# Loading the last tile whole and finishing it in four pieces, in a streaming gradient kernel

## Chip, cores, metric

One core of a Trainium2 chip. The metric is the device time of one execution in microseconds (us). A run more than 1.5% above the fastest of its kernel counts as slow. The experiments ran in three rounds, each on another chip; a ratio compares only runs of one round, while the profiles are compared across them.

## The reference

```python
def setup_inputs():
    return {"x": np.random.randn(8192, 8192).astype(np.float32)}

def reference(x):
    return np.gradient(x, axis=1)
```

Inside a row each result is half the difference of the two neighbours; at the two ends it is the plain difference. 268 MB are read and 268 MB written, with one operation per element: a streaming kernel.

## The kernel before

A tile is two rows per partition, 64 KB per partition and 8 MB in all. There are 32 tiles (0 to 31) and three buffers. SyncE issues the loads, ScalarE the stores, but for those of the last tile, which SyncE issues. GpSimd computes the row ends aside (0.2 us), VectorE does the middle in one instruction (17.2 us), shifted by 64 elements inside the same buffer, and a small copy puts the ends in place. Only the last tile is handled in two rows:

```python
parts = [(ld[k], 0, R)] if i < nsets - 1 else [(ld_rows[r], r, 1) for r in range(R)]
for sem, r0, nr in parts:
    nc.sync.dma_start(out=slots[k][:, SH + r0*m : SH + (r0+nr)*m],
                      in_=x_sets[i, :, r0*m : (r0+nr)*m]).then_inc(sem, 16)
# ... (cut)
if i < nsets - 1:
    ready = put_aside(i, 0, R, ld[k], 16 * ld_n[k])
    work(i, 0, R, ready, placer, nc.scalar, st[k])     # middle, ends, store
else:
    for r in range(R):                                 # last tile, row by row
        ready = put_aside(i, r, 1, ld_rows[r], 16)
        work(i, r, 1, ready, nc.vector, nc.sync, st_rows[r])
```

A load waits for the landing of the load before it and for the store that frees its buffer.

Of the kernel before, what the change touches and what calls it, by code (L numbers as in the profile page):

```python
# [1 line left out]

# [4 lines left out]


@with_exitstack
def kernel(  # L10
    ctx: ExitStack,
    tc: tile.TileContext,
    x: bass.AP,
    out: bass.AP,
):









    nc = tc.nc
    P = nc.NUM_PARTITIONS
    n, m = x.shape
    R = 2
    NB = 3
    SH = 64  # L30
    W = R * m
    nsets = n // (P * R)
    f32 = x.dtype

    x_sets = x.rearrange("(s p t) m -> s p (t m)", p=P, t=R)
    out_sets = out.rearrange("(s p t) m -> s p (t m)", p=P, t=R)

    pool = ctx.enter_context(tc.tile_pool(name="pool", bufs=1))
    slots = [pool.tile([P, SH + W], f32, name=f"slot{k}", tag=f"slot{k}") for k in range(NB)]
    ends = pool.tile([P, nsets, R, 2], f32, name="ends", tag="ends")  # L40

    with tc.tile_critical():  # L42
        ld = [nc.alloc_semaphore(f"ld{k}") for k in range(NB)]
        st = [nc.alloc_semaphore(f"st{k}") for k in range(NB)]
        ld_rows = [nc.alloc_semaphore(f"ld_row{r}") for r in range(R)]
        st_rows = [nc.alloc_semaphore(f"st_row{r}") for r in range(R)]

        aside = [nc.alloc_semaphore("aside"), 0]
        halved = [nc.alloc_semaphore("halved"), 0]
        placed = {  # L50
            nc.vector: [nc.alloc_semaphore("placed_dve"), 0],
            nc.scalar: [nc.alloc_semaphore("placed_act"), 0],
        }

        def done(ins, counter):
            ins.then_inc(counter[0])
            counter[1] += 1
            return counter[0], counter[1]

        ld_n, st_n = [0] * NB, [0] * NB  # L60

        def load(i):
            k = i % NB
            if i < NB:
                parts = [(ld[k], 0, R)]
            else:

                nc.sync.wait_ge(ld[(i - 1) % NB], 16 * ld_n[(i - 1) % NB])
                nc.sync.wait_ge(st[k], 16 * st_n[k])  # L69
                parts = [(ld[k], 0, R)] if i < nsets - 1 else [(ld_rows[r], r, 1) for r in range(R)]  # L70
            for sem, r0, nr in parts:
                nc.sync.dma_start(  # L72
                    out=slots[k][:, SH + r0 * m : SH + (r0 + nr) * m],
                    in_=x_sets[i, :, r0 * m : (r0 + nr) * m],
                ).then_inc(sem, 16)
            ld_n[k] += 1

        def put_aside(i, r0, nr, sem, count):

            k = i % NB  # L80
            xin = slots[k][:, SH + r0 * m : SH + (r0 + nr) * m].rearrange("p (t m) -> p t m", m=m)
            nc.gpsimd.wait_ge(sem, count)
            return done(
                nc.gpsimd.tensor_sub(  # L84
                    out=ends[:, i, r0 : r0 + nr, :],
                    in0=xin[:, :, 1 : m : m - 2],
                    in1=xin[:, :, 0 : m - 1 : m - 2],
                ),
                aside,
            )  # L90

        def work(i, r0, nr, ready, placer, storer, sem):

            b = slots[i % NB]
            c0, c1 = r0 * m + 1, (r0 + nr) * m - 1
            mid = b[:, c0:c1]
            after = b[:, SH + c0 + 1 : SH + c1 + 1]
            before = b[:, SH + c0 - 1 : SH + c1 - 1]
            nc.vector.wait_ge(*ready)

            at = done(
                nc.vector._custom_dve(  # L102
                    dve_ops.TENSOR_TENSOR_REDUCE_SUB_MAX,
                    out=mid,
                    in0=after,
                    in1=before,
                    s0=0.0,
                    s1=0.5,
                ),
                halved,  # L110
            )
            res = b[:, r0 * m : (r0 + nr) * m].rearrange("p (t m) -> p t m", m=m)
            to, of = res[:, :, 0 : m : m - 1], ends[:, i, r0 : r0 + nr, :]
            placer.wait_ge(*at)
            copy = nc.scalar.copy if placer is nc.scalar else nc.vector.tensor_copy
            at = done(copy(out=to, in_=of), placed[placer])  # L116
            storer.wait_ge(*at)
            storer.dma_start(
                out=out_sets[i, :, r0 * m : (r0 + nr) * m],
                in_=b[:, r0 * m : (r0 + nr) * m],  # L120
            ).then_inc(sem, 16)

        for i in range(NB):
            load(i)
        for i in range(nsets):
            k = i % NB
            if i < nsets - 1:
                ready = put_aside(i, 0, R, ld[k], 16 * ld_n[k])
                placer = nc.scalar if i % 2 else nc.vector
                work(i, 0, R, ready, placer, nc.scalar, st[k])  # L130
                st_n[k] += 1
            else:
                for r in range(R):
                    ready = put_aside(i, r, 1, ld_rows[r], 16)
                    work(i, r, 1, ready, nc.vector, nc.sync, st_rows[r])
            if i + NB < nsets:
                load(i + NB)
        for r in range(R):
            nc.sync.wait_ge(st_rows[r], 16)
        for k in range(NB):  # L140
            nc.sync.wait_ge(st[k], 16 * st_n[k])


# [1 line left out]
_INS = ['x']  # L145
_OUTS = [((8192, 8192), 'float32')]


# [23 lines left out]
```

## Time and profile before

| | before |
|---|---|
| time, median of 3 | 1249.37 us (1248.43 to 1249.98) |
| span in the profile | 1246.3 us |
| DMA engines | 99.8% busy, 431 GB/s over the span |
| VectorE | 44% busy |
| last load issued (first row) | 1176.50 us |
| last store issued, landed | 1231.7, 1244.7 us |

To read it: the 16 DMA engines are shared by SyncE's queue (q1: the loads, and at the end the stores of the last tile) and ScalarE's (q10: all other stores), and they are the bound. A transfer is issued when an engine puts it in its queue, and has landed when the last of its completions has come.

One number is used throughout: the **tail**, from the issue of the last load to the end of the span. It is 1246.3 - 1176.5 = 69.8 us here. All kernels below, but for one that is marked, are alike up to that issue, so the tail holds all of the change and leaves out what varies earlier.

### The profile page before, as it was taken

Reading aid. Unit: us, or ns where it says so; the run is one execution under the profiler, and the core shown is the slowest. Engines: PE = TensorE matmul, PEld = TensorE weight load, DVE = VectorE, ACT = ScalarE, POOL = GpSimd, SP = SyncE. Lnnn points to the kernel's source line nnn. Section 1 sums busy time; section 2 is a strip of 40 time slices with the busy share of each in tenths; the row PEclk is TensorE's granted clock in tenths of the full one; section 3 lists DMA queues with packets and bytes.
Section 4 is the critical chain, followed back from the end, with each engine's and each line's share of the span. In section 5 each row is a group of like instructions: output and inputs, shape, how many; then the busy total and the mean of one; then the engine's idle time right before and its main releaser. Section 6 shows DMA issues by size and latency. Waiting matters only on the chain.

```text
span 1246.3 us, 254 instructions
## 1 busy us (share of the span) xinstructions
DVE 554.4 (44%) x51; ACT 4.2 (0%) x16; POOL 6.7 (1%) x37
## 2 busy tenths in 40 slices
DVE  2841552355533455333553345543355433554362
ACT  0000000000000000000000000000000000000000
POOL 0000000000000000000000000000000000000000
DMA  9999999999999999999999999999999999999998
GB/s 404 438 433 421 425 438 435 435 433 438 435 438 435 431 423 433 431 438 438 438 435 438 438 427 427 427 433 435 438 435 423 438 435 433 429 435 427 433 427 379
DMA packets 9504, 536.88 MB, mean 431 GB/s; under 512 B 1056, under 2 KB 1056, under 8 KB 1056
## 3 DMA queue, kind: packets, MB, share of 16 engines
q1 hardware_dynamic: 5040, 276.83, 51.6%
q10 hardware_dynamic: 4464, 260.05, 48.2%
HBM read 268.44 MB, written 268.44 MB: 431 GB/s over the span
## 4 chain that ended last, share of the span: by engine, by line
DMA 97%; DVE 2%; issue 0%; POOL 0%; SPq 0%
DMA slot<-in_x_dram 93%; DMA out_dram<-slot 3%; DVE slot L102 2%; POOL ends L84 0%; DVE slot L116 0%; SPq L72 0%; SPq L167 0%; SPq L69 0%; SPq L42 0%
## 5 line engine op out<-in xcount | busy, mean ns | idle before, releaser
L102 DVE CUSTOM_DVE_ANT_0 slot<-slot 128x16382 f32<-128x16382 f32 (+1 forms) x33 | 551.3, 16706 | 676.7 <-POOL ends L84 676.7
L84 POOL TENSOR_TENSOR ends<-slot 128x4 f32<-128x4 f32 (+1 forms) x33 | 6.5, 198 | 1215.8 <-DMA slot<-in_x_dram 1215.8
L116 ACT COPY slot<-ends 128x4 f32<-128x4 f32 x15 | 3.0, 197 | 1110.2 <-DVE slot L102 1110.2
L116 DVE COPY slot<-ends 128x4 f32<-128x4 f32 (+1 forms) x18 | 3.1, 172 | 0.6
L116 ACT ACT_TABLE_LOAD x1 | 1.3, 1283 | 41.0 <-DVE slot L116 41.0
L156 POOL MEMSET const-bfloat16-1.0<- 128x1 bf16 x1 | 0.1, 101 | 0.0
L156 POOL MEMSET const-uint8-127<- 128x1 uint8 x1 | 0.1, 101 | 0.0
L156 POOL MEMSET const-float32-0.0<- 128x1 f32 x1 | 0.1, 98 | 0.2 <-issue 0.2
L156 POOL MEMSET const-float32-1.0<- 128x1 f32 x1 | 0.1, 98 | 0.0
## 6 DMA issues: line engine op xcount, KB each, us to landing
slot<-in_x_dram SPq DMA_DIRECT2D x2, 4096.0 KB, 32.5
out_dram<-slot SPq DMA_DIRECT2D x2, 4096.0 KB, 21.4
slot<-in_x_dram SPq DMA_DIRECT2D x31, 38.6
out_dram<-slot ACTq DMA_DIRECT2D x31, 37.7
```

The lines of the kernel that those rows point to most:

```text
L84: nc.gpsimd.tensor_sub(out=ends[:, i, r0 : r0 + nr, :], in0=xin[:, :, 1 : m : m - 2], in1=xin[:, :, 0 : m - 1 : m - 2],),
L102: nc.vector._custom_dve(dve_ops.TENSOR_TENSOR_REDUCE_SUB_MAX, out=mid, in0=after, in1=before, s0=0.0, s1=0.5,),
L116: at = done(copy(out=to, in_=of), placed[placer])
L156: nc = _bacc.Bacc("TRN2", target_bir_lowering=False, num_devices=1)
```

## The change

The intent: the two row loads have 32 KB per partition and come off badly beside the 64 KB store of tile 30, so the second half lands late (45.6 us), and 8.7 us of VectorE and a 4 MB store hang from it. One load of 64 KB should get an even share, and four short pieces should leave less behind the landing.

```diff
-                parts = [(ld[k], 0, R)] if i < nsets - 1 else [(ld_rows[r], r, 1) for r in range(R)]
-            for sem, r0, nr in parts:
-                nc.sync.dma_start(...)          # one per row on the last tile
+            nc.sync.dma_start(out=slots[k][:, SH : SH + W], in_=x_sets[i]).then_inc(ld[k], 16)
...
-                for r in range(R):
-                    ready = put_aside(i, r, 1, ld_rows[r], 16)
-                    work(i, r, 1, ready, nc.vector, nc.sync, st_rows[r])
+                step = W // PIECES              # PIECES = 4
+                for q in range(PIECES):
+                    c0, c1 = q * step, (q + 1) * step
+                    row, right = divmod(q, 2)
+                    at = halve(b, c0 + 1 - right, c1 - right, at)
+                    edge = c1 - 1 if right else c0
+                    put = place(nc.scalar, b[:, edge : edge + 1], ends[:, i, row, right : right + 1], at)
+                    store(nc.sync, i, c0, c1, put, st_last[q])
```

With this the edge copies of the last tile go from VectorE to ScalarE, and its ends are put aside by one GpSimd instruction instead of two. The rest of the diff splits a helper in three and moves the closing waits; it changes no other instruction.

More of the change, by code (lines that the diff above doesn't have):

```diff
@@ L31 @@
     W = R * m
+    PIECES = 2 * R
     nsets = n // (P * R)
@@ L44 @@
         st = [nc.alloc_semaphore(f"st{k}") for k in range(NB)]
-        ld_rows = [nc.alloc_semaphore(f"ld_row{r}") for r in range(R)]
-        st_rows = [nc.alloc_semaphore(f"st_row{r}") for r in range(R)]
+        st_last = [nc.alloc_semaphore(f"st_last{q}") for q in range(PIECES)]
         aside = [nc.alloc_semaphore("aside"), 0]
@@ L63, in load, with put_aside @@
             k = i % NB
-            if i < NB:
-                parts = [(ld[k], 0, R)]
-            else:
+            if i >= NB:
                 nc.sync.wait_ge(ld[(i - 1) % NB], 16 * ld_n[(i - 1) % NB])
                 nc.sync.wait_ge(st[k], 16 * st_n[k])
-                parts = [(ld[k], 0, R)] if i < nsets - 1 else [(ld_rows[r], r, 1) for r in range(R)]
-            for sem, r0, nr in parts:
-                nc.sync.dma_start(
-                    out=slots[k][:, SH + r0 * m : SH + (r0 + nr) * m],
-                    in_=x_sets[i, :, r0 * m : (r0 + nr) * m],
-                ).then_inc(sem, 16)
+            nc.sync.dma_start(out=slots[k][:, SH : SH + W], in_=x_sets[i]).then_inc(ld[k], 16)
             ld_n[k] += 1
-        def put_aside(i, r0, nr, sem, count):
+        def put_aside(i):
             k = i % NB
-            xin = slots[k][:, SH + r0 * m : SH + (r0 + nr) * m].rearrange("p (t m) -> p t m", m=m)
-            nc.gpsimd.wait_ge(sem, count)
+            xin = slots[k][:, SH : SH + W].rearrange("p (t m) -> p t m", m=m)
+            nc.gpsimd.wait_ge(ld[k], 16 * ld_n[k])
             return done(
                 nc.gpsimd.tensor_sub(
-                    out=ends[:, i, r0 : r0 + nr, :],
+                    out=ends[:, i, :, :],
                     in0=xin[:, :, 1 : m : m - 2],
@@ L90, in put_aside, with halve @@
             )
-        def work(i, r0, nr, ready, placer, storer, sem):
-            b = slots[i % NB]
-            c0, c1 = r0 * m + 1, (r0 + nr) * m - 1
-            mid = b[:, c0:c1]
-            after = b[:, SH + c0 + 1 : SH + c1 + 1]
-            before = b[:, SH + c0 - 1 : SH + c1 - 1]
+        def halve(b, c0, c1, ready):
             nc.vector.wait_ge(*ready)
-            at = done(
+            return done(
                 nc.vector._custom_dve(
                     dve_ops.TENSOR_TENSOR_REDUCE_SUB_MAX,
-                    out=mid,
-                    in0=after,
-                    in1=before,
+                    out=b[:, c0:c1],
+                    in0=b[:, SH + c0 + 1 : SH + c1 + 1],
+                    in1=b[:, SH + c0 - 1 : SH + c1 - 1],
                     s0=0.0,
@@ L111, in work, with place, store @@
             )
-            res = b[:, r0 * m : (r0 + nr) * m].rearrange("p (t m) -> p t m", m=m)
-            to, of = res[:, :, 0 : m : m - 1], ends[:, i, r0 : r0 + nr, :]
-            placer.wait_ge(*at)
-            copy = nc.scalar.copy if placer is nc.scalar else nc.vector.tensor_copy
-            at = done(copy(out=to, in_=of), placed[placer])
-            storer.wait_ge(*at)
-            storer.dma_start(
-                out=out_sets[i, :, r0 * m : (r0 + nr) * m],
-                in_=b[:, r0 * m : (r0 + nr) * m],
-            ).then_inc(sem, 16)
+        def place(engine, out, in_, ready):
+            engine.wait_ge(*ready)
+            copy = nc.scalar.copy if engine is nc.scalar else nc.vector.tensor_copy
+            return done(copy(out=out, in_=in_), placed[engine])
+        def store(engine, i, c0, c1, ready, sem):
+            engine.wait_ge(*ready)
+            engine.dma_start(out=out_sets[i, :, c0:c1], in_=slots[i % NB][:, c0:c1]).then_inc(sem, 16)
         for i in range(NB):
@@ L126 @@
             k = i % NB
+            b = slots[k]
+            at = put_aside(i)
             if i < nsets - 1:
-                ready = put_aside(i, 0, R, ld[k], 16 * ld_n[k])
-                placer = nc.scalar if i % 2 else nc.vector
-                work(i, 0, R, ready, placer, nc.scalar, st[k])
+                at = halve(b, 1, W - 1, at)
+                rows = b[:, 0:W].rearrange("p (t m) -> p t m", m=m)
+                at = place(nc.scalar if i % 2 else nc.vector, rows[:, :, 0 : m : m - 1], ends[:, i, :, :], at)
+                store(nc.scalar, i, 0, W, at, st[k])
                 st_n[k] += 1
             else:
-                for r in range(R):
-                    ready = put_aside(i, r, 1, ld_rows[r], 16)
-                    work(i, r, 1, ready, nc.vector, nc.sync, st_rows[r])
+                step = W // PIECES
[6 more added lines that the diff above has]
+                    store(nc.sync, i, c0, c1, put, st_last[q])
             if i + NB < nsets:
                 load(i + NB)
-        for r in range(R):
-            nc.sync.wait_ge(st_rows[r], 16)
         for k in range(NB):
             nc.sync.wait_ge(st[k], 16 * st_n[k])
+        for q in range(PIECES):
+            nc.sync.wait_ge(st_last[q], 16)
 _INS = ['x']
```

## The prediction

> **What bounds the kernel now.** I read the page first: the strip of busy tenths, then the queues, then the chain.
>
> ```profile
> DVE  2841552355533455333553345543355433554362
> DMA  9999999999999999999999999999999999999998
> ...
> q1 hardware_dynamic: 5040, 276.83, 51.6%
> q10 hardware_dynamic: 4464, 260.05, 48.2%
> ...
> DMA 97%; DVE 2%; issue 0%; POOL 0%; SPq 0%
> ```
>
> The 16 DMA engines are at the top digit in 39 slices of 40. The two queues' packets fill 51.6 + 48.2 = 99.8% of the engines' span of 1246.3 us, which is 1243.8 us. So only some 2.5 us of DMA idleness exist in the whole run. VectorE is about half busy. The change touches only the end, so the next views are the end of the chain and of the timeline.
>
> ```profile
> 1137.75 38.73 DMA slot<-in_x_dram
> ...
> 1176.88 45.64 DMA slot<-in_x_dram
> 1222.51 0.07 issue
> 1222.58 0.20 POOL ends L84
> 1222.78 0.02 issue
> 1222.81 8.70 DVE slot L102
> ```
>
> A normal load of 64 KB per partition takes 38.7 us from issue to landing. The second half of the last load, only half as large, took 45.6 us, landing at 1222.5. From it hang 0.2 us on GpSimd, 8.7 us of VectorE, 0.17 us of edge copy, and the last store, issued at 1231.7. Read alone, this chain invites the change: an earlier landing and shorter last pieces should shorten a 23 us tail. So the decisive view is whether the DMA engines stand idle during that tail (columns: stretch, its length, DVE, ACT, POOL, clock, DMA share, GB/s).
>
> ```profile
> 1205.00:1222.00 17.00, 0.11 (x1) 0.00 (x0) 0.00 (x0) 1.00 0.96 411
> 1222.00:1232.00 10.00, 8.86 (x2) 0.00 (x0) 0.19 (x1) 1.00 1.02 439
> 1232.00:1240.00 8.00, 0.00 (x0) 0.00 (x0) 0.00 (x0) 1.00 1.00 430
> 1240.00:1246.00 6.00, 0.00 (x0) 0.00 (x0) 0.00 (x0) 1.00 0.43 186
> ```
>
> They don't. While the last 8.7 us of VectorE run, the engines move 439 GB/s: the store of tile 30 and that of the first row are still queued. (0.96 and 1.02 side by side are whole packets booked at one moment; the mean over 1205 to 1240 is 1.0.) Only after 1240 do they run dry: 0.43 of 6 us is 2.6 us of work, so data end near 1242.6 on average over engines, the last store lands at 1231.7 + 13.0 = 1244.7, and the program ends 1.6 us later.
>
> Why the second half-load was slow: the share of the queues from 1198 to 1222.
>
> ```profile
> q10 hardware_dynamic: 106, 6.95, 67.6%
> q1 hardware_dynamic: 106, 3.05, 29.4%
> ```
>
> q10 carries tile 30's store and q1 the row load. Of the page's 9504 packets 66 x 16 = 1056 are the tiny completion packets; the other 8448 = 62 x 128 + 4 x 128 are one packet per partition and transfer: 64 KB for a whole tile, 32 KB for a row. Taking turns packet by packet, the queue with 32 KB packets gets one third: 3.05 against 6.95 MB.
>
> **What the Trainium skill says.** "DMA: Bandwidth & Descriptors", section Queues, rings and completion order: an engine takes turns between the queues that have work, a packet at a time. The 29.4 to 67.6 split above agrees, with its half-sized packets on one side. The same page, Where 436 GB/s comes from, puts the ceiling of the 16 engines at 435 GB/s; the trace shows 434 from 600 to 1100 us. So the kernel is at that ceiling. "Perfetto Trace Analysis", section DMA Optimizations: "If DMA engines are generally idle, splitting DMAs into smaller sections may allow the overall task to complete sooner." Here they aren't idle. "VectorE: DVE Perf Modes", Specifications, gives a 0.96 GHz clock; the two sizes in the trace (16382 elements 17224 ns, 8190 elements 8690 ns) have a slope of 8534 / 8192 = 1.042 ns per element, the same.
>
> **The change part by part.**
>
> *One load instead of two* (one issue of 0.33 us less, under a full queue: worth 0). It has 64 KB packets, so it shares evenly with the stores. When it starts to move, about 3 us after the issue at 1176.5, each engine still has some 2 packets of tile 29's store to do: from 1178 to 1188 that queue's share is 59.0%, or 5.9 us, of which 1 to 1.5 us lie before 1179.5. A 64 KB packet takes 2.42 us (600 to 1100 us: 100.3% of 16 x 500 us over 3725 - 416 packets). Two of ours and two of the store's: 9.7 us, to 1189. Then alone to 1196.5 (tile 30's store is issued at 1194.2, its packets come some 2 us later): 3 more of our 8 packets. The last 3 alternate with 3 of the store: 14.5 us, to 1211. With an uneven finish of engines I expect the landing at 1212 (estimate, 1211 to 1216): 10 us earlier than now.
>
> *VectorE in four pieces of 4095 elements*: 8690 - 4095 x 1.042 = 4424 ns each, 17.7 us in all, against 17.4 for the two of before: 0.3 us more, off the path. The edge copy goes from VectorE (169 ns) to ScalarE (197 ns) for one column: 4 x 0.2 us, beside the next piece. First piece: 1212 + 0.07 + 0.20 + 0.03 + 4.42 + 0.27 = issue at 1217.0; then every 4.45 us, the last at 1230.3, where before it was 1231.7.
>
> *Stores of 16 KB per partition.* A 32 KB packet takes 1.214 us (1226 to 1240: 99.2% of 16 x 14 us over 207 - 24 packets), half of 2.42, so no fixed cost per packet is visible and I take 0.61 us for 16 KB. A piece is 8 packets per engine, 4.9 us; four are 19.5 us, as the two row stores of before were 16 x 1.214 = 19.4. Halving the packets may cost up to 0.01 us each, 0.3 us in all.
>
> *Do the engines run dry before the pieces come?* At 1211 tile 30's store has had 3 of its 8 packets; 5 x 2.42 = 12.1 us remain, to 1223. The first piece is issued at 1217 and moves by 1220. Three us to spare. After that the pieces arrive every 4.45 us and take 4.9 us, so the backlog grows. Nothing runs dry, the engines do the same bytes with the same end near 1242.6 and the same 3.7 us after it.
>
> Sum: load packets 19.4 to 19.4, store packets +0.1 to +0.3, tail 0, idle 0: +0.2 us against an uneven finish of the engines that can move either way by about 1 us. I predict 1249.3.
>
> **The rivals.** *The tail really shortens.* The chain speaks for it: 8.7 us of VectorE become 4.4 and the landing comes 10 us earlier. If the engines were idle meanwhile it would save 5 to 10 us, 1240 to 1244. The share of 1.02 in those very 10 us is against it. At most the 2.5 us of idleness in the whole run could shrink: 1247.
>
> *A new gap.* One load must land whole before anything of the last tile is computed, where before row 0 landed at 1196. If the queues don't share evenly and it lands at 1222 as now, tile 30's store is done when it lands and the engines wait about 4.4 + 0.6 + 2 to 3 us for the first piece: 1255 to 1257. The even 50.6 to 49.7 of the two queues over 600 to 1100 us is against it. Break-even is a landing near 1215 to 1216; each us after it costs one.
>
> *Small packets are dear.* If 16 KB packets took 0.70 us, 32 per engine would add 2.9 us: 1252. The equal rate of 32 and 64 KB packets is against it.
>
> **Range and chances.** The executions of before spread from 1248.4 to 1250.0. With 0.5 us for packets, up to 2 us for a small gap, and 1 to 2 us for a lucky end, I take 1247.3 to 1251.5. Two per cent is 25 us: a saving of that size is ten times the idleness there is, and a loss of it needs a gap three times the worst rival's. So within 2% at 0.98.
>
> **What would show it.** Right: the last load lands near 1212; the four VectorE pieces take 4.42 us; the DMA share stays 1.0 from 1205 to 1240; the last store is issued near 1230 and lands near 1244.7, 14 us later, because it stands in a queue. Wrong: a stretch between 1212 and 1235 with a DMA share clearly under 1 (new gap); a last store that lands within some 7 us of its issue (the chain, not the engines, sets the end); fewer than 425 GB/s while only pieces move (dear packets); or an end before 1242 (idleness that I failed to see).

## The result, and the profile after

The changed kernel took 1248.78 us in the median of 6 runs (1247.55 to 1250.75), beside 1249.58 for the kernel before (1247.92 to 1254.9). The ratio is 0.9991 with a 95% interval of 0.9971 to 1.0011: the same. Ratios here and below are the mean time of one kernel's fast runs over that of the other's of the same rounds, so they are not quite the ratio of the medians.

The end of the chain of waits after (start, length, what):

```profile
1177.10 38.96 DMA slot<-in_x_dram
1216.06 0.07 issue
1216.13 0.21 POOL ends L78
1216.34 0.02 issue
1216.36 4.44 DVE slot L90
```

The last load lands at 1216.06, 39.0 us after its issue; before, the second row landed 1222.5 - 1176.5 = 46.0 us after the first row's issue. The chain got shorter as intended, and the time did not: the span is 1247.0, so the tail is 1247.0 - 1177.1 = 69.9 us, where before it was 69.8. The timeline shows the four pieces and their stores (start, length, then what; an "x4" line runs from the first to the last of four):

```profile
1216.36 17.81 DVE L90 CUSTOM_DVE_ANT_0 slot<-slot 128x4095 f32<-128x4095 f32 x4 [21.55 <-POOL ends L78]
1220.82 0.19 ACT L104 COPY slot<-ends 128x1 f32<-128x1 f32 x1 [64.61 <-DVE slot L90]
1221.04 13.71 SPq L108 DMA_DIRECT2D out_dram<-slot  x4
```

The first store is issued at 1221.04, the last at 1234.4, landing 10.7 us later. The same four stretches as before (length, DVE, ACT, POOL, clock, DMA share, GB/s):

```profile
1205.00:1222.00 17.00, 5.61 (x2) 0.19 (x1) 0.20 (x1) 1.00 1.00 432
1222.00:1232.00 10.00, 9.93 (x3) 0.38 (x2) 0.00 (x0) 1.00 0.92 367
1232.00:1240.00 8.00, 2.17 (x1) 0.19 (x1) 0.00 (x0) 1.00 1.00 430
1240.00:1246.00 6.00, 0.00 (x0) 0.00 (x0) 0.00 (x0) 1.00 0.52 224
```

The engines are full up to 1222 and from 1232 on. In between is a dent (0.92, 367 GB/s). More than half of it is the booking of whole packets where they begin: in the run below with nothing computed, where all four stores are issued before 1219 and no engine pauses, the same stretch reads

```profile
1222.00:1232.00 10.00, 0.00 (x0) 0.00 (x0) 0.00 (x0) 1.00 0.88 375
```

With each packet spread over its own time, it is 403 GB/s here and 432 in that run. In the packet records (the trace, read packet by packet) the 16 KB packets take 0.611 us; but the first one of 14 of the 16 engines took 1.12 to 1.49 us, so these engines lost 0.5 to 0.9 us. They had not run dry, as far as the records show. Every engine goes from its last packet of tile 30's store (these ended at 1222.8 to 1225.4) to the piece without a pause; and in the three runs below where the engines do stand idle when the first piece is issued, its first packets begin 0.8 to 1.0 us after the issue, which would be 1222.0 here. Nor was the piece simply slow to come: in the run "Early landing and delay together" first packets that begin 2.1 to 2.5 us after the issue take 0.61 us, while here those that begin 1.8 to 2.5 us after it are the long ones. In the control run of the same kernel it was 10 engines. Why the first packet is slow, no run here shows.

Why did the load land at 1216 and not at 1212? The load queue in the five stretches 1206 to 1208, to 1210, to 1212, to 1214 and to 1216.5 (packets, MB, share):

```profile
q1 hardware_dynamic: 7, 0.46, 52.9%
q1 hardware_dynamic: 8, 0.00, 0.2%
q1 hardware_dynamic: 7, 0.07, 7.7%
q1 hardware_dynamic: 1, 0.00, 0.0%
q1 hardware_dynamic: 1, 0.00, 0.0%
```

Packets of 0.00 MB are completion packets, of which each of the 16 engines owes one. By 1208 all packets of data but one have begun (a packet is booked where it begins). Then come 8 completions, 6 more with one last packet of data, and one and one in the last two stretches. The packet records give the times: 15 engines ended their data by 1209.7, and their completions started 2.4 us after each one's data, behind one more 64 KB packet of the store (2.42 us). One engine was a round behind: its last data ended at 1213.28, its completion started at 1215.69, and the landing came at 1216.06.

### The profile page after: what moved, and what is told of

The parts are those of the page before. It is cut to its first block, busy times and chain, and to the rows that moved or that the text cites. A ratio compares the mean times of both kernels' runs of the same rounds, so it can differ in the third digit from the quotient of the medians.

```text
span 1247.0 us, 259 instructions
## 1 busy us (share of the span) xinstructions
DVE 554.4 (44%) x51; ACT 5.0 (0%) x20; POOL 6.5 (1%) x36
## 4 chain that ended last, share of the span: by engine, by line
DMA 96%; DVE 3%; issue 0%; POOL 0%; ACT 0%; SPq 0%
DMA slot<-in_x_dram 93%; DMA out_dram<-slot 3%; DVE slot L90 3%; POOL ends L78 0%; ACT slot L104 0%; DVE slot L104 0%; SPq L163 0%; SPq L68 0%; SPq L44 0%
## 5 line engine op out<-in xcount | busy, mean ns | idle before, releaser
L78 POOL TENSOR_TENSOR ends<-slot 128x4 f32<-128x4 f32 x32 | 6.3, 198 | 1209.6 <-DMA slot<-in_x_dram 1209.6
L104 ACT COPY slot<-ends 128x4 f32<-128x4 f32 (+1 forms) x19 | 3.7, 197 | 1188.4 <-DVE slot L90 1188.4
L104 DVE COPY slot<-ends 128x4 f32<-128x4 f32 x16 | 2.7, 172 | 0.5
```

The costliest lines, as they stand in the source:

```text
L78: nc.gpsimd.tensor_sub(out=ends[:, i, :, :], in0=xin[:, :, 1 : m : m - 2], in1=xin[:, :, 0 : m - 1 : m - 2],),
L104: return done(copy(out=out, in_=in_), placed[engine])
```

## The experiments

Two theories ran through all of them. **Theory A**: the end is set by the work queued in the DMA engines; VectorE and the landing of the last load cost nothing as long as the first piece's store comes before the engines run dry. **The rivals**: the chain through VectorE sets the end and some loss cancels its gain, or small packets cost something that cancels it. Edits are shown against the changed kernel, unless said otherwise.

### Only the one load

Against the kernel before:

```diff
-parts = ... [(ld_rows[r], r, 1) for r in range(R)]
+parts = ... [(ld_rows[0], 0, R)]
-ready = put_aside(i, r, 1, ld_rows[r], 16)
+ready = put_aside(i, r, 1, ld_rows[0], 16)
```

> Only the one-piece load of the last tile; compute and store stay two whole rows. Theory A (the DMA engines' queued work sets the end, and compute is free as long as the first store comes before they run dry): the load lands at about 1216, row 0 takes 8.7 us, its store moves at about 1226.5, some 4 us after tile 30's store is done (1222.3); so a gap, and 1.5 to 3 us more than the changed kernel: 1250.5 to 1252. Rival B (the one load gains, since it lands 6 us earlier, and small packets give it back): faster than before by 2 to 6 us, 1243 to 1247.

Measured: 1250.66 us, ratio to before 1.0018 (0.9996 to 1.0040), not told apart from 1. The first row's store is issued 48.0 us after the load, in the packet records every engine stands idle for 0.8 to 2.7 us before it, and yet the tail is 1248.3 - 1178.0 = 70.3 us, only 0.4 over the changed kernel. Rival B (2 to 6 us faster) falls. Theory A's 1.5 to 3 us was too much. This fits a gap borne mostly by engines that would not have ended last: here all 16 end their data between 1246.4 and 1246.6, where in the kernel before they end from 1242.3 to 1244.3.

### Only the four pieces

The two row loads of before stay, each with its own wait; the four pieces wait for the row they lie in, and one wait more keeps the second row's pieces behind the first's. Core of the edit:

```diff
+if i == nsets - 1:
+    for r in range(R): nc.sync.dma_start(... row r ...).then_inc(ld_rows[r], 16)
...
+if not right:
+    nc.vector.wait_ge(*at)
+    at = put_aside_row(i, row)
```

> Only the four pieces; the last tile is loaded in two rows as before. Theory A: the engines are full either way, so as before within 0.7 us (1248.7 to 1250). Rival B (the halved last compute gains 4.4 us): about 1245. Rival C (16 KB packets cost): 1251 or more.

Measured: 1249.89 us, ratio 1.0007 (0.9991 to 1.0024); tail 1246.1 - 1176.0 = 70.1 us. Theory A holds: neither a gain of 4 us from shorter pieces nor a loss from 16 KB packets. Here the packet records show 0.611 us for every first packet of a piece.

### Nothing computed on the last tile

```diff
-at = halve(...); put = place(...); store(nc.sync, i, c0, c1, put, st_last[q])
+nc.sync.wait_ge(ld[k], 16 * ld_n[k])
+nc.sync.dma_start(out=out_sets[i, :, c0:c1], in_=b[:, SH + c0 : SH + c1]).then_inc(st_last[q], 16)
```

> The changed kernel with nothing computed on the last tile: its four pieces are stored straight from where they were loaded, on landing (wrong result in the last tile on purpose). Theory A: 17.8 us of VectorE taken away save no more than the small gap of about 0.7 us: 1248 to 1249. Rival (the chain through VectorE sets the end): 5 to 18 us less, 1231 to 1244.

Measured: 1251.32 us, ratio to before 1.0016 (0.9998 to 1.0033); the result is wrong in the last tile. The timeline has all four stores right after the landing:

```profile
1215.52 2.61 SPq L128 DMA_DIRECT2D out_dram<-slot  x4
```

The first is issued 38.7 us after the load instead of 43.9, the last after 41.0 instead of 57.3, and the tail is 1246.4 - 1176.85 = 69.6 us. Taking the whole compute of the last tile away saved 0.3 us of the tail and nothing of the time. This is the plainest answer to the question where the expected gain went: there was none to have.

### The last tile in one piece

```diff
-for q in range(PIECES): ...           # four pieces
+at = halve(b, 1, W - 1, at)
+at = place(nc.scalar, rows[:, :, 0 : m : m - 1], ends[:, i, :, :], at)
+store(nc.sync, i, 0, W, at, st_last[0])
```

> The changed kernel with the last tile computed and stored in one piece. Theory A: the store moves at about 1216.4 + 17.2 + 1.4 = 1235, the engines run dry at 1222.3, so a gap of 12 to 13 us, less some 1.3 us of lag of the engine that ends last: 1259 to 1261. Rival (bytes alone set the end, gaps get hidden): 1249.

Measured: 1255.87 us, ratio 1.0060 (1.0043 to 1.0077), tail 1253.6 - 1175.15 = 78.5 us. The gap is there, and bytes alone don't set the end:

```profile
1220.00:1224.00 4.00, 4.00 (x1) 0.00 (x0) 0.00 (x0) 1.00 0.23 98
1224.00:1231.00 7.00, 7.00 (x1) 0.00 (x0) 0.00 (x0) 1.00 0.00 0
```

VectorE works through these 11 us while the DMA engines move nothing for seven of them. The size was less than expected (8.6 us in the tail and some 7 in the time, not 10 to 12): the slack is larger than the 1.3 us I had read from how far the last engine's end lies behind the others'. The next runs measure it.

### Delay ahead of the first piece

```diff
+for _ in range(20):                    # and 60
+    nc.gpsimd.wait_ge(*at)
+    at = put_aside(i)
```

> The changed kernel with 20 more of the small GpSimd instructions of 0.2 us ahead of the first piece, about 4.4 us of delay. Theory A: the slack of 1.3 us (leading engines end 1242.4 to 1242.9, the last 1244.1) is used up and the rest is paid: 2.5 to 3.5 us over the changed kernel, 1251.3 to 1252.3. Rival D (there is no slack, the chain sets the end): 4.4 us more, 1253.2. Rival (bytes alone): 0.

> The same with 60, about 13 us of delay. Theory A: 11.5 to 12.3 us over the changed kernel, 1260.3 to 1261.1, so that the slope between 20 and 60 is one and the offset the slack. Rival D: 13 us more.

Measured: 1250.24 us with 20, ratio 1.0009 (0.9987 to 1.0030), which can't tell the theories apart by time; 1261.97 us with 60, ratio 1.0092 (1.0077 to 1.0107). The tails are clearer. The stores of the pieces, with 20 and with 60:

```profile
1224.37 13.71 SPq L108 DMA_DIRECT2D out_dram<-slot  x4
1237.62 13.71 SPq L108 DMA_DIRECT2D out_dram<-slot  x4
```

The last loads were issued at 1174.69 and 1177.22, the spans are 1247.2 and 1260.5. So the first store was issued 49.7 and 60.4 us after the load (43.9 without delay), so the delays were 5.7 and 16.5 us, and the tails grew from 69.9 to 72.5 and 83.3 us. The slope between the two is (83.3 - 72.5) / (60.4 - 49.7) = 1.0, and 3.1 us of each delay were free. So theory A has its two halves in one measurement: rival D (every us is paid) and "bytes alone" (none is) both fall. The slack of the changed kernel is 3.1 us, not 1.3. The packet records say why: the tail grows once the engine that is last to finish tile 30's store runs dry. In the changed kernel that is 48.3 us after the load's issue, and an idle engine takes up the first piece 0.9 us after its issue, so the first store may be issued at 47.4, which is 43.9 and 3.5 us more (an estimate from these numbers; measured 3.1).

### Tile 30's store in four pieces too

```diff
-store(nc.scalar, i, 0, W, at, st[k])
+cuts = PIECES if i == nsets - 2 else 1
+for q in range(cuts): store(nc.scalar, i, q * W // cuts, (q + 1) * W // cuts, at, st[k])
```

> The changed kernel with the store of the last tile but one cut in four as well, so that its packets are 16 KB and its turn is a quarter of the load's. Theory A: the last load lands some 5 to 7 us earlier (1209 to 1211 instead of 1216), the completion packet waits 0.6 us instead of 2.4, the small gap at 1222 goes, and the time is the same within 0.7 us (1248 to 1249.5). Rival (the landing of the last load sets the end): 5 us less, about 1244.

Measured: 1247.82 us, ratio 0.9984 (0.9970 to 0.9997). The landing moved as expected and more, to 1207.8, 31.5 us after the issue, and the completions started 0.60 us after the data instead of 2.4: they do wait for one packet of the other queue, whatever its size. The dent is gone (1.01, 433 GB/s from 1222 to 1232), and the tail is 69.8 us: landing 7 us sooner after the issue bought nothing in it. But the time lay 0.16% under before, so it was run again with the changed kernel as a control:

> The kernel whose tile 30 is stored in four pieces once more, since its first timing was 0.16% under before with an interval that excludes equality, while its tail in the profile was no shorter (69.8 us). Theory A: it was the spread between runs; this time within 0.1% of the changed kernel run here, and the tail 69.8 us again within 0.5. Rival (true gain): 0.1% or more under the changed kernel again.

> The changed kernel once more, unchanged, as a control of the spread beside the next one. Theory A: the tail (from the issue of the last load to the end of the span in the profile) is 69.9 us again within 0.5; the time lies within 0.15% of before, on either side. Rival (the change is a small true gain): under before by 0.1% or more again.

Measured: 1251.04 us, ratio 0.9997 (0.9977 to 1.0018), and for the control 1251.22 us, ratio 1.0002 (0.9982 to 1.0023); tails 70.7 and 70.0 us. The tail of 70.7 is a little outside what I had expected and the 0.16% did not come back. It was spread. The profiles show where the spread sits: the last load was issued anywhere from 1174.7 to 1180.9 us, before anything that was changed runs. In the control the last load landed after 36.7 us, 2.3 us sooner than in the first profile of the same kernel, and the tail was the same.

### Early landing and delay together

The last edit plus the 20 small instructions.

> Tile 30 stored in four pieces, and 20 more of the small GpSimd instructions (5.7 us as measured) ahead of the first piece. In the changed kernel this delay lengthened the tail from 69.9 to 72.5 us. Theory A (an early landing buys slack, not time): the first store is issued some 42 us after the last load, before the break-even of about 47, so the tail is 69.9 within 0.5. Rival (the delay is paid wherever it stands): 72.5.

Measured: 1250.36 us, ratio 0.9994 (0.9976 to 1.0012); the first store is issued 42.3 us after the load and the tail is 1248.6 - 1178.7 = 69.9 us. The same delay that cost 2.6 us of tail costs none here. An early landing buys slack, not time.

### The last load in four pieces, waited for together

```diff
+cuts = PIECES if i == nsets - 1 else 1
+for q in range(cuts): nc.sync.dma_start(... quarter q ...).then_inc(ld[k], 16); ld_n[k] += 1
```

> The changed kernel with the last load cut into four 16 KB pieces, all waited for together. Theory A with turns by packet: the load gets a fifth beside tile 30's store and lands when that is done, 1220 to 1224; the engines then wait some 5 to 6 us for the first piece: 1253 to 1256. Rival (turns by bytes, or the landing doesn't matter): 1249.

Measured: 1258.15 us, ratio 1.0058 (1.0040 to 1.0077), tail 77.3 us. With 16 KB packets the load landed 49.6 us after its issue instead of 39.0, after tile 30's store was done, and the engines waited for the first piece:

```profile
1220.00:1224.00 4.00, 0.00 (x0) 0.00 (x0) 0.00 (x0) 1.00 0.62 254
1224.00:1231.00 7.00, 4.08 (x1) 0.00 (x0) 0.20 (x1) 1.00 0.08 33
```

So the size of the load's packets does matter, once the whole tile is waited for: a single load of 64 KB per partition doesn't cost these 7 us. (The four pieces behind two row loads, each with a wait of its own, cost nothing either, as shown above.)

### Every store in four pieces

This kernel differs from the first tile on, so it has no comparable tail.

```diff
-store(nc.scalar, i, 0, W, at, st[k])
+for q in range(PIECES): store(nc.scalar, i, q * W // PIECES, (q + 1) * W // PIECES, at, st[k])
```

> The changed kernel with the store of every tile cut into four 16 KB pieces. A 16 KB packet took 0.611 us and a 64 KB one 2.418: 32 x 0.611 - 8 x 2.418 = 0.21 us more per tile and engine, 31 tiles: 6.4 us more, 1254.5 to 1256.5, if the engines stay full. Rival (packets of 16 KB cost nothing at scale): 1249. Rival (the loads, which now get four fifths of the turns, outrun the stores and leave gaps): 1262 or more.

Measured: 1290.01 us, ratio 1.0314 (1.0279 to 1.0350): far over the 6.4 us more, and within the last rival's "1262 or more", but without the gaps that it gives as the reason. The queues from 600 to 800 us, then the end of the run:

```profile
q10 hardware_dynamic: 2979, 43.45, 50.7%
q1 hardware_dynamic: 720, 41.94, 49.7%
```

```profile
1260.00:1270.00 10.00, 0.00 (x0) 0.00 (x0) 0.00 (x0) 1.00 0.86 369
1270.00:1280.00 10.00, 0.00 (x0) 0.00 (x0) 0.00 (x0) 1.00 0.07 28
1280.00:1289.00 9.00, 0.00 (x0) 0.00 (x0) 0.00 (x0) 1.00 0.05 22
```

In the packet records of these 200 us a store packet took 0.611 us, as cheap as in the tail; but a 64 KB load packet took 49.7% x 3200 / (720 - 80 completions) = 2.49 us in the mean, where before it was 2.42. And at the end a share of 0.05 to 0.07 is one engine of 16 (0.0625) working alone: 14 engines end their data at 1268.5 to 1268.8, one at 1270.9, the last at 1287.4. So the cost at scale shows in slower loads and in one engine that falls behind, not in the time of a small packet. Why the loads slow down and why one engine falls behind, no run here shows.

### All tails in one table

| kernel | first store of the last tile, us after its load was issued | tail, us | first store + 22.8 |
|---|---|---|---|
| before | 28.6 (half of the tile) | 69.8 | |
| only four pieces | 24.5 (a quarter) | 70.1 | |
| tile 30 in four, twice | 36.5, 37.3 | 69.8, 70.7 | 59.3, 60.1 |
| nothing computed | 38.7 | 69.6 | 61.5 |
| changed, twice | 43.9, 41.7 | 69.9, 70.0 | 66.7, 64.5 |
| tile 30 in four, delay 20 | 42.3 | 69.9 | 65.1 |
| only one load | 48.0 | 70.3 | 70.8 |
| delay 20 | 49.7 | 72.5 | 72.5 |
| last load in four | 54.6 | 77.3 | 77.4 |
| one piece | 56.4 | 78.5 | 79.2 |
| delay 60 | 60.4 | 83.3 | 83.2 |

The 22.8 is taken from the two delay runs. The tail is the larger of two numbers: some 70 us of queued transfers, or the first store plus 22.8 us. They cross at 47.2. (The 22.8 agrees with its parts in the run with 20: 0.9 us until the first packet begins, 19.7 us of pieces, 2.2 us from the last data to the end of the span.) Each row is one profile. The last load in four pieces and the kernel in one piece were not used for the 22.8 and fit within 0.1 and 0.7 us.

## Why the prediction was right

**The time** was 1249.3 predicted and 1248.78 measured, in the range of 1247.3 to 1251.5, and "within 2%" had 0.98. The mechanism, engines that are full whatever VectorE does, is shown from both sides: taking the compute away gains nothing, and delaying it costs nothing until 47 us and one for one after. That the two numbers lie within 0.5 us of each other is luck: the same kernel had a median of 1251.22 in the control round. What was predicted and shown is that nothing changes.

**The one load.** An even share beside the stores came as predicted (packets of the two queues alternate on each engine), but the landing did not: 1212 was predicted, 1216.06 measured, just past the edge of the estimate. Set against the issue, 35.5 us were predicted; 39.0 and, in the control, 36.7 were measured. The step that failed is "The last 3 alternate with 3 of the store: 14.5 us, to 1211. With an uneven finish of engines I expect the landing at 1212". On 15 engines not three packets of the store came before the load's last one, but one (8 engines) or two (7), so their data were in 28.9 to 32.6 us after the issue, where 34.5 were predicted: this term was too large. (Its two starts were off in the trace of before already: there the first row load's packets begin 4.1 to 6.0 us after its issue, not 3, and those of tile 30's store 3.4 to 4.6 us after its own, not 2.) Two were missing or too small, and outweighed it: the last engine did alternate with three and came 3.6 us after the others (36.2), where 1 us was allowed for an uneven finish, and its completion waited for one more packet of the store (2.4 us).

**VectorE.** 4424 ns per piece predicted, 4426 measured; off the path, as said.

**The stores.** 0.61 us per 16 KB packet predicted, 0.611 measured; dear packets are out for the tail. Cutting every store cost 3.1%, which none of the prediction's steps would have given.

**"Nothing runs dry"** held, as far as the records show. It rested on a first piece that moves at 1220, three us before tile 30's store ends at 1223. The piece was issued 4 us later than predicted, at 1221.0, and could have moved at 1222.0 (0.9 us after its issue, as on idle engines, instead of the 3 predicted), so part of one error was taken back by the other; the engines finished tile 30's store at 1222.8 to 1225.4, so 0.8 us or more were to spare. What was not foreseen is the slow first packet, 0.5 to 0.9 us on 14 engines. It cost nothing to be seen in the tail (69.9 against 69.8): the engine that ended last was not among those 14. Its share of tile 30's store had its completion only at 1226.0, and it ended at 1244.8, where the others were done by 1243.6.

**Break-even** was put at a landing near 1215 to 1216, and "each us after it costs one". The slope is right (1.0), the place was 3 us too early: 47.2 us less the 5.0 us from landing to first store is 42.2 us after the issue, on the prediction's clock 1218.7.

**The signs to look for.** The last store was issued at 1234.4 rather than 1230, and landed 10.7 us later rather than 14; more than the 7 us that would have meant a chain-bound end. The sign of a new gap, a share clearly under 1 between 1212 and 1235, did come up (0.92 from 1222 to 1232), and was not one: the run without compute shows 0.88 there. The rival "the tail really shortens" is refuted by the run without compute; the rival "a new gap" did not come true in this kernel but is exactly what the last load in four pieces does.

## What to carry to other kernels

At the end of a run that is bound by DMA, a chain of load, compute and store looks long and invites cutting; first read whether the DMA engines are busy beside it. In these runs the work that hangs from the last load was free until the queue ran empty; one experiment that removes it and one that delays it found that point. Small effects are best read from a stretch that begins where the change begins: the tails of the two kernels that were profiled twice repeat within 0.1 and 0.9 us, where whole executions differ by several.

## What the Trainium skill lacked or had wrong

- "DMA: Bandwidth & Descriptors", section Queues, rings and completion order, tells of turns by packet. It gives no time for a completion that waits behind another queue: a load's completion packet started 2.4 us after the engine's last data, behind one 64 KB packet of the other queue, and 0.60 us behind a 16 KB one. Nor does it say what follows for shares: one packet per partition made 32 KB against 64 KB a split of 29.4 to 67.6%, and 16 KB packets moved the landing of an 8 MB load from 39.0 to 49.6 us.
- The same page, section Rules for kernel authors, asks for at least 1 MiB per DMA for full bandwidth. Stores of 2 MiB with 16 KB per partition, on all tiles, made the kernel 3.1% slower than 8 MiB ones (427 GB/s from 600 to 800 us, where the kernel before had 434 from 600 to 1100).
- No page that I read tells how far the engines drift apart when two hardware queues stream together: one engine lagged by 3.6 us at the last load of the changed kernel, and one worked alone for 16.6 us at the end of the run with every store cut, 18.7 us after 14 others had ended. The trace doesn't name the engine.
